# VectorE's share of the adaLN modulation as product-and-sum with a row of silu(c), and VectorE work per slot charged by durations

## The chip, the core and the metric

The kernel runs on one core of one Trainium2 chip. The metric is the device time of one execution in microseconds (us), lower is better. TensorE multiplies, VectorE and ScalarE work on tiles of 128 partitions, GpSimd is hardly used, and SyncE issues the weight loads from device memory.

## The reference, cut to what matters

Two layers; each has a token mixer (sparse attention, an S5 state-space branch, a pooling branch, merged by gates) and a convolutional FFN. Both sub-layers are modulated by shift, scale and gate vectors, which come from one vector c by a large matrix-vector product: per layer 6 parts of 2048 numbers.

```python
mod = silu(c) @ w_ada[l] + b_ada[l]        # (2048) x (2048, 12288), f32
sh1, sc1, g1, sh2, sc2, g2 = split(mod, 6)
h = rms_norm(x, g_norm1) * (1 + sc1) + sh1
x = x + g1 * hybrid_mixer(h, ...)          # attention, s5_mixer, pool_mixer, gates, w_out
h = rms_norm(x, g_norm2) * (1 + sc2) + sh2
x = x + g2 * conv_ffn(h, ...)
# in s5_mixer: y = gelu(scan(...)); y = y * sigmoid(y @ w_glu)
```

## The kernel before, in words

The large weights come as a stream of 936 slots, tiles of 128 x 1024 f32, in one order written out ahead. For each slot ScalarE makes a rounded copy (`whi`, `make_hi`), VectorE the remainder (`wlo`, `make_lo`), and TensorE multiplies: in the usual full slot eight 512-column matmuls with `whi` (line 326), then eight 256-column ones with `wlo` (line 331). There are three `wlo` buffers, so the `wlo` of slot s+2, which is made at the start of slot s, waits until TensorE is done with slot s-1. A slot is counted here by its `wlo` instruction.

All else is issued between slots by `step()`. Evacuations of finished outputs always run. Tasks are generators, stepped in a fixed order: first the low list (the modulation), then pooling, indexing, attention, and last S5 (`s5_task`). A task goes on only while `credit` > 0 (`step_task`, line 197). `credit` gains a fixed amount per slot (in proportion to its width) and is held between -2 and 2; every VectorE instruction, `wlo` and evacuations too, is charged by a formula in its helper (`tt`, `stt`, `ts`, `vcopy`). A piece that yields None ends the task's turn for that slot. If the stream comes to a block whose input isn't ready, `require()` steps the task that provides it at once and without regard to credit; everything it issues then stands ahead of that block on the engines' queues.

S5 has per layer 16 state groups in eight pairs: tables (`tb`, built by doubling on ScalarE and VectorE), two products of 512 columns, two of 256, two scans, three last products for each group, then matmuls (`prod,cc`). Every two pairs end in a tail (gelu, `yt`). The result y feeds the GLU (`w_glu`), at slot 160 in layer 0 and at slot 629 in layer 1. S5's tables of constants (`s5_prepare`, many short instructions) must be complete when the mixer opens (`open_mixer`, slot 37 in layer 0).

The modulation has 384 tiles of 128 x 1024 (`adaw`), loaded on SyncE's queue like the stream's weights; the list `ADA` sets their order and `ADA_PLAN` how many may be used by which slot (`ada_early`). 192 of them go through TensorE (`ada_group` with `on_pe`): four chunks side by side in one matmul step, not charged to credit, then a ScalarE copy `acc`, column transposes (line 569), small adds. The other 192 go through VectorE: per tile two passes `acc = w * c + acc` of 512 columns, and per eight tiles four transposes on TensorE and a reduction of their columns (line 545). The first 64 tiles use a ring of eight buffers, the later ones four.

Of the kernel before, what the change touches and what calls it, by code (L numbers as in the profile page):

```python
# [37 lines left out]
SLOT = 1024  # L38
NRAW, NHI, NLO, NADA, APRE = 4, 4, 3, 4, 4

# [39 lines left out]

ADA_PLAN = ((0, 18), (8, 34), (18, 50), (30, 66), (48, 66), (140, 128), (204, 160), (296, 192), (460, 296), (580, 320), (670, 356), (770, 384))


ADA = [(0, [(1, t), (0, t)], 2 if t < 4 else 4, True) for t in (0, 2, 4, 8, 12)]
for _l in range(DEPTH):
    if _l:
        ADA += [(_l, [(p, t + j) for j in (0, 4) for p in (1, 0)], 4, False) for t in (0, 8)]
    ADA += [(_l, [(2, t) for t in range(0, 16, 4)], 4, not _l)]
    ADA += [(_l, [(p, t + j) for j in (0, 4) for p in (4, 3)], 4, not _l or t == 0) for t in (0, 8)]
    ADA += [(_l, [(5, t) for t in range(0, 16, 4)], 4, False)]  # L90

# [29 lines left out]
class Kernel:  # L121
    def __init__(self, ctx, tc, a):
        self.tc, self.nc, self.a = tc, tc.nc, a
        nc = self.nc
        self.cpool = ctx.enter_context(tc.tile_pool(name="cpool", bufs=1))
        self.spool = ctx.enter_context(tc.tile_pool(name="spool", bufs=1))
        self.hpool = ctx.enter_context(tc.tile_pool(name="hpool", bufs=1))
        self.epool = ctx.enter_context(tc.tile_pool(name="epool", bufs=1))
        self.psum = ctx.enter_context(tc.tile_pool(name="psum", bufs=1, space=PSUM))
        self.slots = []  # L130
        self.tasks, self.low, self.evacs, self.fresh = [], [], [], []
        self.done = set()
        self.credit = 0.0
        self.acredit = 0.0
        self.banks = list(range(8))
        self.left = 0
        self.raw, self.hi, self.lo = {}, {}, {}
        self.slot_no = 0
        self.ada_tiles, self.ada_next, self.ada_on_pe = {}, 0, True
        dpool = ctx.enter_context(tc.tile_pool(name="dpool", bufs=1, space=bass.MemoryType.DRAM))  # L140
        self.x_save = dpool.tile([128, KT, T], F32, name="x_save")
        ctx.enter_context(tc.manual_schedule())

# [8 lines left out]
    def tt(self, out, a, b, op):  # L152
        self.credit -= 0.069 + 1.04e-3 * self.size(out)
        self.nc.vector.tensor_tensor(out, a, b, op=op)  # L154

    def stt(self, out, a, s, b, op0, op1):
        self.credit -= (0.069 if isinstance(s, float) else 0.13) + 1.04e-3 * self.size(out)
        self.nc.vector.scalar_tensor_tensor(out, a, s, b, op0=op0, op1=op1)  # L158

    def ts(self, out, a, s1, s2, op0, op1=None):  # L160
        self.credit -= 0.069 + 0.7e-3 * self.size(out)
        if op1 is None:
            self.nc.vector.tensor_scalar(out, a, s1, None, op0=op0)
        else:
            self.nc.vector.tensor_scalar(out, a, s1, s2, op0=op0, op1=op1)

    def vcopy(self, out, a):
        self.credit -= 0.069 + 0.7e-3 * self.size(out)
        self.nc.vector.tensor_copy(out, a)
# [209 lines left out]
    def run_stream(self):  # L379
        n = len(self.slots)  # L380
        for s in range(n):
# [6 lines left out]
            o.emit(self.hi.pop(s), self.lo.pop(s))  # L388
            self.credit = max(min(self.credit + 2.6 * o.w / SLOT, 2.0), -2.0)
            self.acredit = max(min(self.acredit + 2.6 * o.w / SLOT, 2.0), -2.0)  # L390
            self.step()
# [99 lines left out]
    def ada_fetch(self, upto):  # L491
        while self.ada_next < upto:
            i = self.ada_next
            pool, bufs = self.ada_ring if i < 64 and i % (NADA + APRE) < APRE else (self.cpool, NADA)
            t = pool.tile([128, 1024], F32, name="adaw", tag="adaw", bufs=bufs)
# [4 lines left out]
    def ada_group(self, i0, l, chunks, wt, on_pe, ahead, last):  # L500

        def mine(i, n):
            self.ada_fetch(min(i + n, last))
            return [self.ada_tiles.pop(i + j) for j in range(n)]
        m = len(chunks)
        self.ada_on_pe = on_pe
        if on_pe:
            b, ps = yield from self.take_bank()

            i, n, width = i0, wt // 2, 128 * wt  # L510
            for q in range(0, KT, 4 // m):
                ws = mine(i, n)
                for g in range(4):
                    k = q + g // m
                    cs = self.cact[:, k:k + 1].to_broadcast([128, 32])
                    w = ws[g * n // 4][:, g * width % 1024:][:, :width]
                    self.mm(ps[32 * g:32 * g + 32, :width], cs, w, start=q == 0, stop=q + 4 // m == KT)
                i += n
                self.ada_fetch(min(i + ahead, last))
                while self.ada_early(i):  # L520
                    yield None
                yield 1
        else:
            for g in range(m):
                acc = self.cpool.tile([128, 512], F32, name="acc", tag="acc", bufs=1)
                for q in range(8):
                    i = i0 + 8 * g + q
                    self.ada_fetch(min(i + ahead, last))
                    w, = mine(i, 1)
                    for k in range(2):  # L530
                        wk = w[:, k * 512:(k + 1) * 512]
                        cs = self.cact[:, 2 * q + k:2 * q + k + 1]
                        if q == 0 and k == 0:
                            self.ts(acc, wk, cs, None, OP.mult)
                        else:
                            self.stt(acc, wk, cs, acc, OP.mult, OP.add)
                        yield 1
                    while self.ada_early(i + 1):
                        yield None
                yield None  # L540
                b, cols = yield from self.ada_columns(acc, 4)
                part, t = chunks[g]
                mod = self.mod[l][:, 16 * part + t:16 * part + t + 4]
                self.credit -= 0.6
                self.nc.vector.reduce_sum(mod, cols, axis=AX.X)
                self.free_bank(b)
                self.ada_done(l, part, t, mod)
            return
        yield None
# [14 lines left out]
        yield None  # L564

    def ada_columns(self, acc, wt):
        b, ps = yield from self.take_bank()
# [11 lines left out]
    def ada_task(self, lo, hi, ahead, last):  # L579
        i = sum(2 * wt * len(chunks) for _, chunks, wt, _ in ADA[:lo])  # L580
        for l, chunks, wt, on_pe in ADA[lo:hi]:
            yield from self.ada_group(i, l, chunks, wt, on_pe, ahead, last)
            i += 2 * wt * len(chunks)
# [241 lines left out]
    def index_task(self, t):  # L825
# [34 lines left out]
        for r in range(TOPK // 8):  # L860
            self.nc.vector.max(m8, src)
            self.nc.vector.match_replace(wk[r % 2], m8, src, MARK)
            self.credit -= 2 * (0.069 + 1.04e-3 * nk)
            src = wk[r % 2]
# [7 lines left out]
    def attention_task(self, part):  # L872
# [7 lines left out]
        for t in range(2):  # L880
# [3 lines left out]
            for g in range(part, H // per, 2):  # L884
# [11 lines left out]
                self.free_bank(b)  # L896
                self.credit -= 0.6
                self.nc.vector.reduce_max(mxv[:, 0], lg, axis=AX.X)
# [154 lines left out]
    def s5_task(self):  # L1053
# [3 lines left out]
        for j in range(4):  # L1057
# [3 lines left out]
            for i0 in (0, 2):  # L1061
# [11 lines left out]
                for i, tb, (b, bu) in zip((i0, i0 + 1), tbs, bus):  # L1073
# [9 lines left out]
                    rb = p5.r[:, 4 * j + i:4 * j + i + 1].to_broadcast([128, T])  # L1083
                    self.credit -= 0.68
                    for c in range(2):
# [418 lines left out]
    def run(self):  # L1504
# [30 lines left out]
        self.ada_ring = pre, APRE  # L1535
        self.ada_fetch(APRE + NADA)
# [4 lines left out]
        self.norm(0, 1, self.x)  # L1541
        self.rope_tables(pre, posi)
        for s in range(3):
# [13 lines left out]
    def first_ada(self):  # L1557
        yield from self.ada_task(0, 2, APRE + NADA, 16)
        yield from self.ada_task(2, 5, APRE + NADA, 64)
        while ("open", 0) not in self.done:  # L1560
            yield None
        self.ada_fetch(64 + NADA)
        for _ in range(6):
# [49 lines left out]

def _ada(w, chunks, wt, by_k):

    w = w.reshape(KT, 128, 6, 2048)
    x = np.stack([w[:, :, part, 128 * t:128 * (t + wt)] for part, t in chunks])
    x = x.transpose(1, 0, 2, 3) if by_k else x
    return x.reshape(-1, 8 // wt, 128, 128 * wt).transpose(0, 2, 1, 3).reshape(-1, 128, 1024)
# [7 lines left out]
def _arrays(i):  # L1627
# [5 lines left out]
    o["pos"] = i["positions"][0].reshape(2, 128).T  # L1633
    o["w_ada"] = np.concatenate([_ada(i["w_ada"][l], chunks, wt, on_pe) for l, chunks, wt, on_pe in ADA])
    vecs, lvecs = [], []
# [75 lines left out]
```

## Time and profile before

| what | value |
|---|---|
| median of 3 runs | 2960.53 us (2960.5 to 2961.41) |
| profiled execution | 2961.13 us, span of its profile 2959.3 us |
| TensorE matmul busy | 2871.8 us, 97% |
| VectorE busy | 2316.7 us, 78% |
| ScalarE busy | 1385.9 us, 47% |
| mean granted clock of TensorE | 0.988 |

The span runs from the first to the last instruction of the profiled execution. Busy time is the time in which an engine works on at least one instruction; instructions of one engine overlap a little. PE is TensorE, DVE is VectorE, ACT is ScalarE; L154 is line 154 of the kernel printed above.

### The profile page before, as it was taken

The page shows a single profiled execution, that of the slowest core. Times are in us where ns is not written, and L with a number is a line of the kernel's source. Part 1 is how long each engine was busy: PE and PEld are TensorE (multiplying, and loading weights), DVE is VectorE, ACT ScalarE, POOL GpSimd, SP SyncE. Part 2 cuts the span into 40 slices and gives each one's busy share as a digit, 9 for nine tenths or more (in the row PEclk, how much of TensorE's full clock was granted, in tenths as well). Part 3 has the DMA queues.
Part 4 walks back from the last instruction along what each step waited for, and adds up shares of the span by engine and source line. Part 5 has one row for each costly group of instructions (what it writes and reads, how often), then busy time and mean ns, then how long its engine had stood idle before and what let it go on. Part 6 is the DMA issues. An engine that isn't in the chain of part 4 may idle for free.

```text
span 2959.3 us, 45094 instructions
## 1 busy us (share of the span) xinstructions
PE 2871.8 (97%) x16880; PEld 2431.4 (82%) x16880; DVE 2316.7 (78%) x4222; ACT 1385.9 (47%) x2209; POOL 43.6 (1%) x74
## 2 busy tenths in 40 slices
PE   6999999979999999999989999999999999999998
PEld 3787787758788888888868788888888888888887
DVE  5888677766698899999966887899888887556664
ACT  3355544434455543455434455555445554345542
POOL 0000000000000000000000000000000000000000
PEclk9999999989999999999999999999999999999999
DMA  9967767747677778888885555576676776555554
GB/s 368 351 221 254 239 235 259 247 144 277 207 257 252 254 274 295 294 283 302 299 300 198 197 180 181 192 244 239 246 267 207 241 236 204 187 191 187 189 193 151
DMA packets 195387, 705.97 MB, mean 239 GB/s; under 512 B 22496, under 2 KB 23008, under 8 KB 195168
## 3 DMA queue, kind: packets, MB, share of 16 engines
q1 hardware_dynamic: 190656, 691.23, 68.1%
q0 software_dynamic: 3648, 11.01, 1.0%
q8 instruction: 132, 2.16, 0.3%
q10 hardware_dynamic: 864, 0.86, 0.1%
q14 instruction: 87, 0.71, 0.1%
HBM read 698.82 MB, written 4.19 MB: 238 GB/s over the span
## 4 chain that ended last, share of the span: by engine, by line
PE 86%; issue 7%; DVE 5%; DMA 1%; ACT 0%; POOL 0%; POOLq 0%; SPq 0%; DVEq 0%; ACTq 0%
PE b L326 45%; PE b L331 23%; PE b L179 11%; PE b L355 6%; DVE wlo L154 2%; DMA adaw<-in_w_ada 1%; DVE acc L158 1%; PE b L569 0%; DVE prod L154 0%; DVE x L158 0%; POOL out L1497 0%; PE b L913 0%; DVE th L158 0%; DVE ftmp L154 0%; DVE m L154 0%
## 5 line engine op out<-in xcount | busy, mean ns | idle before, releaser
L154 DVE TENSOR_TENSOR wlo<-raw,whi 128x1024 fp32r<-128x1024 f32 x936 | 1136.9, 1215 | 509.9 <-PE b L331 252.8
L174 ACT ACTIVATE whi<-raw 128x1024 fp32r<-128x1024 f32 x936 | 980.8, 1052 | 914.3 <-PE b L326 443.7
L326 PE MATMUL b<-h,whi 128*128 128x512 f32 x4352 | 1104.5, 396 | 4.3 <-DVE h L158 4.3
L326 PEld LDWEIGHTS b<-h,whi 128*128 128x128 f32 x4352 | 784.6, 189 | 178.0 <-issue 18.7
L331 PEld LDWEIGHTS b<-h,wlo 128*128 128x128 f32 x4352 | 594.8, 191 | 43.7 <-DVE wlo L154 0.7
L331 PE MATMUL b<-h,wlo 128*128 128x256 f32 x4352 | 607.6, 282 | 0.3 <-DVE wlo L154 0.3
L326 PE MATMUL b<-hid,whi 128*128 128x512 f32 x1376 | 345.8, 393 | 3.2 <-DVE hid L158 3.2
L326 PEld LDWEIGHTS b<-hid,whi 128*128 128x128 f32 x1376 | 247.4, 189 | 49.1 <-DVE hid L158 4.1
L158 DVE SCALAR_TENSOR_TENSOR acc<-adaw,cact,acc 128x512 f32<-128x512 f32 x360 | 269.3, 748 | 5.2
L331 PEld LDWEIGHTS b<-hid,wlo 128*128 128x128 f32 x1376 | 187.6, 190 | 14.0 <-DVE wlo L154 0.7
L331 PE MATMUL b<-hid,wlo 128*128 128x256 f32 x1376 | 192.0, 282 | 0.3 <-DVE wlo L154 0.3
L179 PE MATMUL b<-whi,h 128*128 128x512 f32 (+1 forms) x512 | 155.2, 376 | 0.0
L326 PE MATMUL b<-mh,whi 128*128 128x512 f32 x512 | 130.7, 397 | 4.1 <-DVE mh L154 4.1
L174 ACT ACTIVATE fth<-ft 128x256 f32<-128x256 f32 x86 | 36.0, 418 | 199.1 <-DVE ft L158 199.1
L179 PE MATMUL b<-adaw,cact 128*32 128x512 f32 (+1 forms) x832 | 111.1, 582 | 9.0 <-DMA adaw<-in_w_ada 9.0
L179 PEld LDWEIGHTS b<-whi,h 128*128 128x128 f32 x512 | 94.1, 188 | 27.9 <-issue 9.5
L326 PEld LDWEIGHTS b<-mh,whi 128*128 128x128 f32 x512 | 92.6, 190 | 26.9 <-ACT whi L174 3.4
L179 PE MATMUL b<-wlo,h 128*128 128x512 f32 (+1 forms) x256 | 95.0, 371 | 0.0
L355 PE MATMUL b<-h,whi 128*128 128x256 f32 x384 | 78.1, 299 | 10.5 <-ACT whi L174 5.5
L174 ACT ACTIVATE hid<-ft 128x256 fp32r<-128x256 f32 x86 | 35.9, 418 | 108.9 <-DVE ft L154 108.9
L158 DVE SCALAR_TENSOR_TENSOR ft<-fa,lvecs,ft 128x255 f32<-128x255 f32 (+1 forms) x172 | 82.5, 481 | 3.0
L355 PEld LDWEIGHTS b<-h,whi 128*128 128x128 f32 x384 | 65.4, 205 | 15.7 <-ACT whi L174 6.6
(262 smaller groups left out, 2548.8 us busy)
## 6 DMA issues: line engine op xcount, KB each, us to landing
adaw<-in_w_ada SPq DMA_DIRECT2D x384, 512.0 KB, 5.5
raw<-in_w_up SPq DMA_DIRECT2D x344, 512.0 KB, 3.7
raw<-in_w_gate SPq DMA_DIRECT2D x192, 512.0 KB, 3.9
raw<-in_w_down_a SPq DMA_DIRECT2D x88, 512.0 KB, 3.5
raw<-in_w_down_b SPq DMA_DIRECT2D x84, 512.0 KB, 3.7
raw<-in_w_out SPq DMA_DIRECT2D x64, 512.0 KB, 4.4
raw<-in_w_q SPq DMA_DIRECT2D x32, 512.0 KB, 3.8
raw<-in_p_a SPq DMA_DIRECT2D x32, 512.0 KB, 4.4
```

What stands on the lines that cost most here:

```text
L154: self.nc.vector.tensor_tensor(out, a, b, op=op)
L158: self.nc.vector.scalar_tensor_tensor(out, a, s, b, op0=op0, op1=op1)
L174: self.nc.scalar.activation(out, a, func, bias=bias, scale=scale)
L179: self.nc.tensor.matmul(out, lhsT, rhs, start=start, stop=stop)
L326: self.nc.tensor.matmul(u.ps, hi[:, j * 128:(j + 1) * 128], x, start=u.cnt == 0, stop=False, skip_group_check=True)
L331: self.nc.tensor.matmul(u.ps[:, T:], lo[:, j * 128:(j + 1) * 128], x[:, :T], start=False, stop=last, skip_group_check=True)
L355: self.nc.tensor.matmul(ps, w, r, start=first and i == 0 and not u.after, stop=last and i == 2 and not u.before, skip_group_check=shared)
```

## The change

For VectorE's 192 tiles the weights are laid out transposed: output columns in partitions, 1024 of the 2048 inputs along the row. silu(c) is spread over all partitions as a row of 2048 by 16 small matmuls at the start, copied by ScalarE and stored in device memory (1 MB); half of it (512 KB) is loaded into one buffer whenever the half changes, seven times in all. One product-and-sum instruction per tile (`ada_sums`) gives 128 outputs' sums over 1024 inputs and adds them to the bias or to the first half's result; transposes, reduction and adds go. TensorE's groups with four chunks take half the width (`wt` 2), so a step uses one tile where it used two. After the first 64 tiles there are three tile buffers where there were four; the eighth of the first ring is the row's. The charges of VectorE instructions are raised, the slot's gain goes from 2.6 to 2.75, and the plan is adapted.

```diff
-NRAW, NHI, NLO, NADA, APRE = 4, 4, 3, 4, 4
+NRAW, NHI, NLO, NADA, APRE = 4, 4, 3, 3, 4
-ADA_PLAN = (..., (140, 128), (204, 160), (296, 192), (460, 296), (580, 320), (670, 356), (770, 384))
+ADA_PLAN = (..., (140, 128), (204, 160), (300, 192), (460, 288), (560, 310),
+            (660, 352), (765, 384))
...
+ADA = [(0, [(1, t), (0, t)], 2 if t < 4 else 4, None) for t in (0, 2, 4, 8, 12)]
+ADA += [(0, [(2, t + j) for j in (0, 2, 4, 6)], 2, None) for t in (0, 8)]
+ADA += [(0, [(p, t + j) for j in (0, 2) for p in (4, 3)], 2, None) for t in (0, 4, 8, 12)]
+ADA += [(0, [(5, t) for t in range(16)], 1, 0)]
+ADA += [(1, [(p, 8 * h + j) for j in range(8) for p in (1, 0)], 1, 1 - h) for h in range(2)]
+ADA += [(1, [(2, t) for t in range(16)], 1, 1)]
+ADA += [(1, [(p, t + j) for j in (0, 2) for p in (4, 3)], 2, None) for t in (0, 4)]
+ADA += [(1, [(p, 8 + j) for j in range(8) for p in (4, 3)], 1, 0)]
+ADA += [(1, [(5, t) for t in range(16)], 1, 1)]
...
     def tt(self, out, a, b, op):
-        self.credit -= 0.069 + 1.04e-3 * self.size(out)
+        self.credit -= 0.155 + 1.04e-3 * self.size(out)
     def stt(self, out, a, s, b, op0, op1):
-        self.credit -= (0.069 if isinstance(s, float) else 0.13) + 1.04e-3 * self.size(out)
+        self.credit -= (0.155 if isinstance(s, float) else 0.215) + 1.04e-3 * self.size(out)
     def ts(self, out, a, s1, s2, op0, op1=None):
-        self.credit -= 0.069 + 0.7e-3 * self.size(out)
+        self.credit -= (0.16 if isinstance(s1, float) else 0.215) + 0.55e-3 * self.size(out)
     def vcopy(self, out, a):
-        self.credit -= 0.069 + 0.7e-3 * self.size(out)
+        self.credit -= 0.15 + 0.6e-3 * self.size(out)
...
-            self.credit = max(min(self.credit + 2.6 * o.w / SLOT, 2.0), -2.0)
-            self.acredit = max(min(self.acredit + 2.6 * o.w / SLOT, 2.0), -2.0)
+            self.credit = max(min(self.credit + 2.75 * o.w / SLOT, 2.0), -2.0)
+            self.acredit = max(min(self.acredit + 2.75 * o.w / SLOT, 2.0), -2.0)
...
+    def ada_sums(self, i0, l, tiles, first, ahead, last):
+        i = i0
+        for h in (first, 1 - first):
+            self.ada_on_pe = False
+            if self.crow_half != h:
+                self.crow = self.cpool.tile([128, 1024], F32, name="crow", tag="crow", bufs=1)
+                self.nc.gpsimd.dma_start(self.crow, self.c_rows[:, h * 1024:(h + 1) * 1024])
+                self.crow_half = h
+                for _ in range(4):
+                    yield None
+            for part, t in tiles:
+                self.ada_fetch(min(i + ahead, last))
+                w = self.ada_tiles.pop(i)
+                n = 16 * part + t
+                col = self.mod[l][:, n:n + 1]
+                seed = self.vec(l, "b_ada")[:, n:n + 1] if h == first else col
+                self.credit -= 0.16 + 1.04e-3 * 1024
+                self.nc.vector.tensor_tensor_reduce(w, w, self.crow, 1.0, seed, OP.mult, OP.add, col)
+                if h != first:
+                    self.done.add(("mod", l, part, t))
+                i += 1
+                yield 1
+                while self.ada_early(i):
+                    yield None
...
+    def start_rows(self):
+        self.rows = []
+        for k in range(KT):
+            if k % 4 == 0:
+                self.rows.append(self.mm_bank())
+            self.mm(self.rows[-1][1][:, k % 4 * 128:k % 4 * 128 + 128], self.cact[:, k:k + 1].to_broadcast([128, 128]),
+                    self.ident)
+    def save_rows(self):
+        t = self.mx.tile([128, 2048], F32, name="rows", tag="oa")
+        for j, (b, ps) in enumerate(self.rows):
+            self.act(t[:, 512 * j:512 * j + 512], ps, AF.Copy)
+            self.free_bank(b)
+        self.nc.gpsimd.dma_start(self.c_rows, t)
+        self.crow_half = None
...
-            self.credit -= 2 * (0.069 + 1.04e-3 * nk)
+            self.credit -= 2 * (0.16 + 1.04e-3 * nk)
...
-                    self.credit -= 0.68
+                    self.credit -= 1.35
```

## Rows read from the trace of the kernel before

**Rows 1.** The page, part 1 (busy, share) and part 6 (KB, us to landing).

```profile
PE 2871.8 (97%) x16880; PEld 2431.4 (82%) x16880; DVE 2316.7 (78%) x4222; ACT 1385.9 (47%) x2209; POOL 43.6 (1%) x74
...
adaw<-in_w_ada SPq DMA_DIRECT2D x384, 512.0 KB, 5.5
```

**Rows 2.** Windows: length, PE, PEld, DVE, ACT, POOL busy (count), PEclk, DMA share, GB/s.

```profile
1100.00:1200.00 100.00, 99.68 (x575) 87.55 (x574) 96.88 (x187) 36.13 (x35) 0.00 (x0) 1.00 0.82 303
2500.00:2600.00 100.00, 100.00 (x573) 87.94 (x573) 56.33 (x64) 37.60 (x37) 0.00 (x0) 1.00 0.59 190
...
0.00:100.00 100.00, 71.77 (x472) 46.57 (x473) 61.57 (x229) 34.70 (x63) 2.14 (x7) 0.95 0.91 355
```

**Rows 3.** Waits of PE: us in total, times, longest.

```profile
PE b L179 <- DVE prod L154: 15.7, 4, 7.4
```

**Rows 4.** Timeline of PE from 1324 us: start, length, instructions merged [idle before].

```profile
1327.68 1.11 PE L331 MATMUL b<-h,wlo 128*128 128x256 f32 x8
1328.64 0.60 PE L569 MATMUL b<-const,acc 128*128 128x128 f32 x4
...
1330.92 1.12 PE L331 MATMUL b<-h,wlo 128*128 128x256 f32 x8
...
1333.71 1.12 PE L331 MATMUL b<-h,wlo 128*128 128x256 f32 x8
```

**Rows 5.** Timeline of PE from 447.6 us, a modulation step between two slots.

```profile
450.50 1.11 PE L331 MATMUL b<-h,wlo 128*128 128x256 f32 x8
451.55 1.06 PE L179 MATMUL b<-adaw,cact 128*32 128x512 f32 x8
...
454.49 1.11 PE L331 MATMUL b<-h,wlo 128*128 128x256 f32 x8
```

**Rows 6.** Timeline of PE from 34.5 us, a modulation group of half width.

```profile
35.75 3.66 PE L179 MATMUL b<-adaw,cact 128*32 128x256 f32 x64
39.34 0.50 PE L179 MATMUL b<-whi,h 128*128 128x512 f32 x1
```

**Rows 7.** Timeline of PE from 1517 us, the first steps of layer 1's group.

```profile
1519.52 1.11 PE L331 MATMUL b<-hid,wlo 128*128 128x256 f32 x8
...
1525.38 1.05 PE L179 MATMUL b<-adaw,cact 128*32 128x512 f32 x4 [2.90 <-DMA adaw<-in_w_ada]
...
1538.54 1.11 PE L331 MATMUL b<-hid,wlo 128*128 128x256 f32 x8
```

**Rows 8.** DVE's groups by form over the span: count, busy us, mean ns.

```profile
L154 DVE TENSOR_TENSOR wlo<-raw,whi 128x1024 fp32r<-128x1024 f32 x920 | 1123.8, 1222 | 498.9 <-PE b L331 252.8 <-issue 139.9 <-ACT fa L174 30.4
L158 DVE SCALAR_TENSOR_TENSOR acc<-adaw,cact,acc 128x512 f32<-128x512 f32 x360 | 269.3, 748 | 5.2
...
L1086 DVE TENSOR_TENSOR_SCAN prod<-r,prod 128x256 f32<-128x256 f32 x64 | 40.5, 675 | 0.0
```

**Rows 9.** Windows of the `wlo` instructions alone: length, DVE busy (count), PEclk, DMA.

```profile
175.33:606.76 431.43, 149.69 (x123) 1.00 0.72 247
1613.60:2067.80 454.20, 171.01 (x141) 1.00 0.62 206
```

**Rows 10.** Timeline of PE from 2060 us, S5's last matmuls in layer 1.

```profile
2065.81 1.91 PE L179 MATMUL b<-prod,cc 128*32 128x256 f32 x14 [0.60 <-DVE prod L154]
```

**Rows 11.** Timeline of DVE from 600 us, S5's rest in layer 0.

```profile
607.91 0.75 DVE L154 TENSOR_TENSOR prod<-prod 128x256 f32<-128x256 f32 x2
...
614.46 0.24 DVE L158 SCALAR_TENSOR_TENSOR tb<-tb,nsn,pr 128x16 f32<-128x16 f32 x1 [3.08 <-ACT pr L174]
...
626.84 1.14 DVE L154 TENSOR_TENSOR prod<-prod,tb 128x256 f32<-128x256 f32 x2
631.70 0.48 DVE L158 SCALAR_TENSOR_TENSOR yt<-u,lvecs,b 128x256 f32<-128x256 f32 x1 [3.71 <-PE b L179]
```

**Rows 12.** PE's groups by form over the span, S5's matmuls of both layers (16 pairs).

```profile
L179 PE MATMUL b<-prod,cc 128*32 128x256 f32 x256 | 36.2, 410 | 15.7 <-DVE prod L154 15.7
...
L179 PE MATMUL b<-u,bp 32*128 32x256 f32 x128 | 18.9, 403 | 0.1
```

More of the change, by code (lines that the diff above doesn't have):

```diff
@@ L79 @@
 FIRST = 48
[L81 to L90, printed above, removed]
+ADA_PLAN = ((0, 18), (8, 34), (18, 50), (30, 66), (48, 66), (140, 128), (204, 160), (300, 192), (460, 288), (560, 310),
+            (660, 352), (765, 384))
[8 more added lines that the diff above has]
+ADA += [(1, [(5, t) for t in range(16)], 1, 1)]
+ADA_FIRST = 64
 EARLY = ("oa", "big8", "qiT", "u", "m2k0", "m2k1", "pt0", "pt1")
@@ L141, in __init__ @@
         self.x_save = dpool.tile([128, KT, T], F32, name="x_save")
+        self.c_rows = dpool.tile([128, 2048], F32, name="c_rows")
         ctx.enter_context(tc.manual_schedule())
@@ L493, in ada_fetch @@
             i = self.ada_next
-            pool, bufs = self.ada_ring if i < 64 and i % (NADA + APRE) < APRE else (self.cpool, NADA)
-            t = pool.tile([128, 1024], F32, name="adaw", tag="adaw", bufs=bufs)
+            r = i % (APRE + NADA + 1) if i < ADA_FIRST else APRE
+            if r == APRE + NADA:
+                t = self.cpool.tile([128, 1024], F32, name="adaw", tag="crow", bufs=1)
+            else:
+                pool, bufs = self.ada_ring if r < APRE else (self.cpool, NADA)
+                t = pool.tile([128, 1024], F32, name="adaw", tag="adaw", bufs=bufs)
             self.nc.sync.dma_start(t, self.a["w_ada"][i])
@@ L498, in ada_fetch @@
             self.ada_next += 1
-    def ada_group(self, i0, l, chunks, wt, on_pe, ahead, last):
-        def mine(i, n):
-            self.ada_fetch(min(i + n, last))
[L504 to L539, printed above, removed]
-                yield None
[L541 to L548, printed above, removed]
@@ new lines, in ada_group @@
+    def ada_group(self, i0, l, chunks, wt, ahead, last):
+        m = len(chunks)
+        self.ada_on_pe = True
+        b, ps = yield from self.take_bank()
+        i, n, width = i0, wt // 2, 128 * wt
+        for q in range(0, KT, 4 // m):
+            self.ada_fetch(min(i + n, last))
+            ws = [self.ada_tiles.pop(i + j) for j in range(n)]
+            for g in range(4):
+                k = q + g // m
+                cs = self.cact[:, k:k + 1].to_broadcast([128, 32])
+                w = ws[g * n // 4][:, g * width % 1024:][:, :width]
+                self.mm(ps[32 * g:32 * g + 32, :width], cs, w, start=q == 0, stop=q + 4 // m == KT)
+            i += n
+            self.ada_fetch(min(i + ahead, last))
+            while self.ada_early(i):
+                yield None
+            yield 1
@@ L564, in ada_group @@
         yield None
+    def ada_sums(self, i0, l, tiles, first, ahead, last):
[9 more added lines that the diff above has]
+            for part, t in tiles:
+                self.ada_fetch(min(i + ahead, last))
+                w = self.ada_tiles.pop(i)
[7 more added lines that the diff above has]
+                i += 1
+                yield 1
+                while self.ada_early(i):
+                    yield None
[13 more added lines that the diff above has]
+        self.crow_half = None
     def ada_columns(self, acc, wt):
@@ L580, in ada_task @@
         i = sum(2 * wt * len(chunks) for _, chunks, wt, _ in ADA[:lo])
-        for l, chunks, wt, on_pe in ADA[lo:hi]:
-            yield from self.ada_group(i, l, chunks, wt, on_pe, ahead, last)
+        for l, chunks, wt, first in ADA[lo:hi]:
+            if first is None:
+                yield from self.ada_group(i, l, chunks, wt, ahead, last)
+            else:
+                yield from self.ada_sums(i, l, chunks, first, ahead, last)
             i += 2 * wt * len(chunks)
@@ L896, in attention_task @@
                 self.free_bank(b)
-                self.credit -= 0.6
+                self.credit -= 0.69
                 self.nc.vector.reduce_max(mxv[:, 0], lg, axis=AX.X)
@@ L1535, in run @@
         self.ada_ring = pre, APRE
-        self.ada_fetch(APRE + NADA)
+        self.ada_fetch(APRE + NADA + 1)
+        self.start_rows()
         for k in range(KT):
@@ L1541, in run @@
         self.norm(0, 1, self.x)
+        self.save_rows()
         self.rope_tables(pre, posi)
@@ L1557, in first_ada @@
     def first_ada(self):
-        yield from self.ada_task(0, 2, APRE + NADA, 16)
-        yield from self.ada_task(2, 5, APRE + NADA, 64)
+        yield from self.ada_task(0, 2, APRE + NADA + 1, 16)
+        yield from self.ada_task(2, 5, APRE + NADA + 1, ADA_FIRST)
         while ("open", 0) not in self.done:
             yield None
-        self.ada_fetch(64 + NADA)
+        self.ada_fetch(ADA_FIRST + NADA)
         for _ in range(6):
@@ L1611, in _wide, with _ada @@
     return np.ascontiguousarray(x.reshape(npc, per, 128, n).transpose(0, 2, 1, 3))
-def _ada(w, chunks, wt, by_k):
+def _ada(w, chunks, wt, first):
+    if first is not None:
+        w = w.reshape(2, 1024, 6, 16, 128)
+        return np.stack([w[h, :, part, t].T for h in (first, 1 - first) for part, t in chunks])
     w = w.reshape(KT, 128, 6, 2048)
-    x = np.stack([w[:, :, part, 128 * t:128 * (t + wt)] for part, t in chunks])
-    x = x.transpose(1, 0, 2, 3) if by_k else x
+    x = np.stack([w[:, :, part, 128 * t:128 * (t + wt)] for part, t in chunks]).transpose(1, 0, 2, 3)
     return x.reshape(-1, 8 // wt, 128, 128 * wt).transpose(0, 2, 1, 3).reshape(-1, 128, 1024)
@@ L1633, in _arrays @@
     o["pos"] = i["positions"][0].reshape(2, 128).T
-    o["w_ada"] = np.concatenate([_ada(i["w_ada"][l], chunks, wt, on_pe) for l, chunks, wt, on_pe in ADA])
+    o["w_ada"] = np.concatenate([_ada(i["w_ada"][l], chunks, wt, first) for l, chunks, wt, first in ADA])
     vecs, lvecs = [], []
```

## The prediction

> **What bounds the kernel now.** I read the page first: TensorE is busy for 97% of the span and VectorE for 78% [rows 1]. Then the windows: in a stretch where VectorE is 97% busy TensorE gets through 575 matmuls in 100 us, in one where VectorE is 56% busy through 573 [rows 2]. So in the FFN a busy VectorE costs nothing: TensorE sets the pace, and what VectorE saves there is not time. Next the waits of TensorE: the largest is 15.7 us on `prod`, the state-space task (S5) of layer 0 [rows 3]. So the question for each edit is: does it change TensorE's instructions, or what TensorE waits for where the stream meets a task that isn't done?
>
> **TensorE's instructions.** *Transposes.* 24 groups of four column transposes (one per VectorE chunk of eight tiles) go. A slot with such a group runs from lo to lo in 3.24 us, the next, plain one in 2.79 [rows 4]: 0.44 us each, -10.6 us. The eight short TensorE groups that stay have two transposes where four had four: +0.9 by the same price.
>
> *Steps of one tile.* The four TensorE groups with four chunks (128 tiles) worked in 64 steps of two tiles; now eight groups work in 128 steps of one. A slot with a two-tile step takes 454.49 - 450.50 = 3.99, so 1.20 more than a plain one [rows 5]. Sixteen tiles at half width in one run take 39.34 - 35.75 = 3.59 for eight steps of two chunks, 0.43 to 0.45 per tile [rows 6], so of the 1.20 about 0.34 is the price of coming and going. If each of the 64 extra steps stood alone: +22. Some fall together (after a group's evacuation the plan has moved two or three tiles on) or beside other small matmuls; half of that rebate leaves +16.5 (8 to 22).
>
> *The late group.* At 1520 us the layer-1 group starts eight tiles behind its plan, so five steps are issued in one slot, each waiting for its tiles: lo to lo 19.02 us against 2.79 + 5 x 1.20 [rows 7], so 10.3 lost. The new plan has 288 tiles at slot 460, where this group begins, and by the charges below VectorE can about keep it (0.6 tiles x 1.28 in 2.75 - 1.22 - 0.77 of a slot of the up-projection): -10.3 (0 if it falls behind in the pauses for the row).
>
> *Start.* 16 small matmuls and four ScalarE copies lie under the wait for x and the first tiles. The row's store adds 1 MB where DMA is 91% busy at 355 GB/s [rows 2]: 0 to 3, taken +2. The seven later row loads stand on GpSimd's queue, each behind the last sum that reads the old half; behind them stand only the small S5 and pool loads, x, x_save and the rsqrt, and none of these is due then. The first sum after a load comes four slots (11 us) on; such a 512 KB load lands in 5.5 [rows 1]. Three tile buffers for four: a load is asked two sums ahead, over three slots (9 us) at 0.6 tiles per slot, also above 5.5; SyncE's wait for that buffer stands before weight loads that wait for a later `wlo` anyway. Nothing for either, unless sums bunch: then `wlo` queues behind a late sum and TensorE behind that.
>
> **The new VectorE sum.** No row shows it. At least it costs what a 1024-wide two-input pass does, 1.22 (`wlo`), at most two of these, 2.44 [rows 8]. It has two fp32 inputs, as the 512-wide `acc` pass has (748 ns, 1.04 ns an element beyond 0.215), so I take 1.28; two such passes and a share of the reduction are replaced, some 0.25 us a tile. That is 47 us of VectorE work, and by rows 2 worth nothing by itself. [...]
>
> **The charges.** This is the largest part. A task's next piece is issued only while `credit` > 0. Until now a slot brought 2.6 and an instruction was charged less than it takes; now a slot brings 2.75 and the charges equal the durations (scan pair 0.68 before, 1.35 now, measured 2 x 675 ns; `wlo` 1.134 before, 1.220 now, measured 1222) [rows 8]. S5 gains least: a pair of state groups has 16 `tb` passes of 16 to 128 columns, and for each of two groups two 512-wide and two 256-wide products, two scans, and three last products: 10.7 by the old charges, 14.6 by the new; a tail per four groups 1.3 and 1.6. Eight pairs and four tails per layer: 91 before, 123.5 now.
>
> *Layer 1, slots 488 to 628* (141 `wlo` [rows 9]). Old supply 141 x 2.6 = 367, spent whole; less `wlo` 160 and S5 91, other work was 116. That is mostly 256-wide passes, 0.335 before and 0.421 now: 145; 35 `acc` passes and their ends in it (31) become some 19 sums (23): 138. New supply 388, less `wlo` 172, less 138: 78 for S5's 123.5. So 45 is left when the stream reaches the GLU, which needs y; before nothing was left, TensorE waited 0.60 us for the last `prod` [rows 10]. *Layer 0, slots 37 to 159* (123 [rows 9]): old supply 319, `wlo` 139; S5 had 76, since the trace shows 14.7 (20 by the new charges) drained at the GLU from 607.9 on [rows 11]; other work 103, now 130. New supply 337 - 150 - 130 = 58: 66 left against 20, +46; if some 12 of the old supply was lost at the cap of 2 (attention waits between 326 and 369 us), +31. I take +38 and, by the same doubt, 41 for layer 1 (35 to 45).
>
> What is left is issued at once when the GLU asks for it, behind a `wlo` that waits for the slot before, so TensorE stands. There a pair takes from 611.4, before the 3.08 wait of `tb`, to 628.0: 16.6 us [rows 11]. Its matmuls (2.26 + 1.18 per pair [rows 12]) then cost the stream nothing: 13.2 net. A tail takes from 628.0 to 634.2 with its 3.71 wait for TensorE, some 4.4 beyond its charge. Layer 0: 38/14.6 = 2.6 pairs, 34, and half a tail more: +36 (28 to 45). Layer 1: 41/14.6 = 2.8 pairs, 37, and a tail more: +42 (32 to 48). *S5's tables* of layer 0 are due when the mixer opens at slot 37, after 33 slots worth 31 full ones. They are short passes, by the two price lists 22 before and 36 now; old supply 81 less `wlo` 35 and 22 leaves 24 of other work, about 32 now; 86 - 38 - 32 = 16 for 36. 17 to 20 is left, in passes that overlap, with three slots of `wlo` already made as cover (10 us): +3 (0 to 11).
>
> What is late next: VectorE now idles some 0.3 us of each mixer slot while S5 waits for credit. Nothing later gives this back, since the output projection needs all of it.
>
> **Sum.** -10.6 + 0.9 + 16.5 - 10.3 + 2 + 36 + 42 + 3 = +79.5 on the profiled execution's 2961.1 (span 2959.3 and 1.8 around it): 3040.6; the median lies 0.6 below that execution: **3040**. All low ends give +48 (3009), all high ends +119 (3080).
>
> **Rivals.** *The charges don't hold S5* (the other side): if S5 is held by banks and its chain through TensorE and ScalarE, not by credit, then the GLU waits as long as before; -10.6 + 0.9 + 16.5 - 10.3 + 2 = -1.5, 2959, and with the extra steps at 8 us 2951. It decides once less than about 9 us of work is added at the two GLUs. Against it: the gaps in VectorE's work of the mixers are small while S5 has work, and S5 ends just in time in layer 1 as a supply that is spent whole would make it. *Half of it*: attention, which stands ahead of S5, leaves slack that S5 takes up, or one layer alone waits: +40 - 1.5, about 3000. [...]
>
> **How the numbers follow.** Forecast 0.72; half of it 0.10; slow sum 0.06; charges that hold nothing 0.12, of which 0.07 faster and 0.05 within 0.2% (6 us, about what a measurement of this kernel tells from no change). So slower 0.88. 2990 to 3085 holds the forecast's bounds and most of the half case, and leaves out the rest.
>
> **What would show it.** Right: TensorE's wait on `prod` grows from 15.7 to some 70 us, in stands of about 70 us before the GLU of layer 0 and 50 before that of layer 1, with several pairs of groups in each; VectorE less busy in the mixers before them; 32 column transposes for 128; a slot with a one-tile step at 3.56; no 19 us slot before layer 1; 192 sums of about 1.28. Wrong: the last scans of a layer close before its GLU as now; sums near 2.4 and `wlo` among TensorE's waits; the layer-1 group late again.

## The result, and the profile of the changed kernel

The changed kernel takes 3071.07 us (median of 4 runs, 3068.71 to 3072.53) against 2960.55 for the kernel before, measured beside it: ratio 1.0372 (95% interval 1.0354 to 1.039). The forecast was slower, 3040, in 2990 to 3085: the sign and the range held, the point was 31 us short.

The page, parts 1 and 5, of the changed kernel (count, busy us, mean ns, idle time before):

```profile
PE 2909.7 (95%) x17328; PEld 2454.6 (80%) x17328; DVE 2285.2 (74%) x4190; ACT 1393.1 (45%) x2217; POOL 48.0 (2%) x82
...
L567 DVE CUSTOM_DVE_ANT_0 adaw<-adaw,crow,mod 128x1024 f32<-128x1024 f32 x96 | 122.5, 1279 | 10.0 <-DMA adaw<-in_w_ada 9.7
...
L186 PE MATMUL b<-prod,cc 128*32 128x256 f32 x256 | 48.4, 481 | 71.7 <-DVE prod L161 71.7
```

VectorE is less busy than before, 74% for 78%, and so is TensorE, 95% for 97% [rows 1]. L567 is the new sum. Its groups by form say what VectorE's instructions cost:

```profile
L161 DVE TENSOR_TENSOR wlo<-raw,whi 128x1024 fp32r<-128x1024 f32 x920 | 1124.5, 1223 | 606.4 <-PE b L338 271.6 <-issue 198.9 <-ACT whi L181 31.7
...
L1115 DVE TENSOR_TENSOR_SCAN prod<-r,prod 128x256 f32<-128x256 f32 x64 | 40.5, 674 | 0.0
...
L567 DVE DVE_READ_ACCUMULATOR2_ANT mod<- 128x1 f32 x192 | 15.8, 82 | 0.0
```

The durations of before stand unchanged (1222 and 675 ns [rows 8]): these VectorE instructions did not become slower. What changed is who waits. The waits of TensorE (us in total, times, longest), where before had 15.7 in 4 for `prod` [rows 3]:

```profile
PE b L186 <- DVE prod L161: 71.7, 13, 10.1
PE b L186 <- DVE wlo L161: 10.1, 1, 10.1
PE b L186 <- DMA adaw<-in_w_ada: 9.2, 13, 3.1
PE b L186 <- ACT pt L181: 7.6, 5, 3.1
...
PE b L942 <- DVE lg L170: 5.0, 3, 2.7
```

To find where, I cut the span at the same `wlo` passes in every kernel (the pass for slot s + 2 opens slot s). These are the windows of the `wlo` passes alone of the changed kernel from slot 0 on, cut at slots 36, 38, 96, 100, 160, 162, 208, 463, 466, 628 and 630: length, VectorE busy with `wlo` (count), granted clock, DMA share, GB/s.

```profile
31.07:172.24 141.17, 41.58 (x38) 0.97 0.85 329
172.24:191.00 18.76, 2.06 (x4) 0.90 0.49 171
191.00:392.36 201.36, 70.25 (x58) 0.98 0.70 236
392.36:432.58 40.22, 4.91 (x4) 0.75 0.33 108
432.58:645.94 213.36, 73.33 (x61) 0.98 0.72 242
645.94:717.44 71.50, 2.45 (x2) 0.62 0.06 23
717.44:865.41 147.97, 56.35 (x46) 1.00 0.76 257
865.41:1590.38 724.97, 311.33 (x255) 0.99 0.82 280
1590.38:1600.04 9.66, 3.67 (x3) 1.00 0.93 342
1600.04:2127.61 527.57, 194.74 (x162) 0.99 0.65 211
2127.61:2190.09 62.48, 2.44 (x3) 0.62 0.07 23
2190.09:3070.19 880.10, 372.11 (x304) 0.99 0.66 213
```

The table gives the length of each stretch before and, for the changed kernel and six of the experiments, how much longer it is.

| slots | before, us | changed | charges only | early rate | old charges | mixer rate | old modulation | rate steps |
|---|---|---|---|---|---|---|---|---|
| start to 36 | 172.7 | -0.4 | -0.7 | +1.5 | +0.3 | +0.9 | +1.3 | +3.0 |
| 36 to 38 (tables) | 6.5 | +12.2 | +12.2 | -0.3 | 0.0 | -0.3 | -0.3 | -0.3 |
| 38 to 96 | 204.7 | -3.4 | -8.5 | +5.9 | +5.1 | +6.4 | +3.3 | +11.4 |
| 96 to 100 (oc) | 15.7 | +24.5 | +17.5 | +8.6 | +2.0 | +9.9 | -0.9 | +4.1 |
| 100 to 160 | 207.1 | +6.2 | -4.4 | +7.0 | +11.5 | +12.0 | +1.1 | +13.1 |
| 160 to 162 (GLU) | 36.6 | +34.9 | +33.4 | +8.0 | -3.5 | -23.3 | -18.8 | -30.2 |
| 162 to 208 | 143.5 | +4.4 | +2.3 | +5.7 | +3.8 | +3.4 | +0.2 | +3.4 |
| 208 to 463 (FFN) | 733.8 | -8.9 | -3.9 | -8.8 | -1.0 | -8.1 | -3.1 | -9.1 |
| 463 to 466 | 24.6 | -14.9 | -16.2 | -15.7 | -16.2 | -15.4 | -16.2 | -14.3 |
| 466 to 628 | 520.3 | +7.2 | +20.6 | +8.6 | +8.9 | +19.2 | +30.3 | +19.3 |
| 628 to 630 (GLU) | 11.1 | +51.4 | +68.2 | +50.8 | +0.7 | -7.5 | +0.3 | -7.7 |
| 630 to end | 882.6 | -2.5 | -2.3 | -2.8 | -1.4 | +0.1 | +0.8 | -0.3 |
| span | 2959.3 | +110.9 | +118.1 | +68.2 | +10.3 | -2.5 | -1.9 | -7.7 |

Four places make +123 in the changed kernel: slot 37, where S5's tables are due, slots 96 to 100, where the stream needs the pools' `oc`, and the two GLUs, which need S5's y. A fifth stand hides in the stretch from 466 to 628, slot 548, where the stream needs layer 1's `oc`. Windows of the `wlo` pass that opens it, first in the kernel before, then in the changed one:

```profile
1819.47:1823.99 4.52, 1.23 (x1) 1.00 0.63 221
...
1867.16:1884.99 17.83, 1.22 (x1) 0.90 0.24 86
```

It is 13.3 us longer. The whole stretch grew by 7.2 alone; what S5 has not issued by slot 628 does not take TensorE's time there. TensorE at the first GLU:

```profile
645.77 0.62 PE L186 MATMUL b<-prod,cc 128*32 128x256 f32 x2
650.60 2.83 PE L186 MATMUL b<-prod,cc 128*32 128x256 f32 x14 [4.20 <-DVE prod L161]
...
662.05 1.06 PE L186 MATMUL b<-prod,cc 128*32 128x256 f32 x2 [6.62 <-DVE prod L161]
666.63 3.62 PE L186 MATMUL b<-prod,cc 128*32 128x256 f32 x14 [3.51 <-DVE prod L161]
...
681.64 1.06 PE L186 MATMUL b<-prod,cc 128*32 128x256 f32 x2 [9.38 <-DVE prod L161]
686.21 3.27 PE L186 MATMUL b<-prod,cc 128*32 128x256 f32 x14 [3.51 <-DVE prod L161]
...
698.12 1.06 PE L186 MATMUL b<-prod,cc 128*32 128x256 f32 x2 [7.58 <-DVE prod L161]
702.69 3.56 PE L186 MATMUL b<-prod,cc 128*32 128x256 f32 x14 [3.51 <-DVE prod L161]
708.82 0.39 PE L362 MATMUL b<-yh,whi 128*128 128x256 f32 x1 [2.56 <-ACT yh L181]
```

Each pair of state groups ends with one `x14`; four fall into the stand, the first partly made before it. A pair takes 16.0 us (650.60 to 666.63) to 16.5 (686.21 to 702.69), as [rows 11] priced it (16.6). How much of S5 is left at a GLU can be counted by its scans, four per pair and 32 per layer. Windows of the scans alone (VectorE busy, count) at the two GLUs, first in the kernel before, then in the changed one:

```profile
606.77:643.35 36.58, 3.80 (x6) 0.72 0.13 44
2065.67:2076.75 11.08, 0.00 (x0) 1.00 0.32 96
...
645.94:717.44 71.50, 8.86 (x14) 0.62 0.06 23
2127.61:2190.09 62.48, 7.60 (x12) 0.62 0.07 23
```

So 3.5 pairs are left at layer 0's GLU where 1.5 were, and 3 at layer 1's where none was.

### The profile page after: what moved, and what is told of

It reads as the page before. It is cut to its first block, busy times and chain, and to the rows that moved or that the text cites. A ratio compares the mean times of both kernels' runs of the same rounds, so it can differ in the third digit from the quotient of the medians.

```text
span 3070.2 us, 45972 instructions
## 1 busy us (share of the span) xinstructions
PE 2909.7 (95%) x17328; PEld 2454.6 (80%) x17328; DVE 2285.2 (74%) x4190; ACT 1393.1 (45%) x2217; POOL 48.0 (2%) x82
## 4 chain that ended last, share of the span: by engine, by line
PE 88%; DVE 5%; issue 3%; ACT 1%; DMA 1%; POOL 0%; POOLq 0%; ACTq 0%; SPq 0%; DVEq 0%
PE b L333 47%; PE b L338 24%; PE b L186 11%; PE b L362 5%; DVE prod L161 1%; DVE wlo L161 1%; DMA adaw<-in_w_ada 1%; DVE prod L1115 1%; DVE tb L165 0%; DMA raw<-in_w_qi 0%; ACT pr L181 0%; POOL out L1526 0%; DVE m L161 0%; PE b L942 0%; DVE prod L165 0%
## 5 line engine op out<-in xcount | busy, mean ns | idle before, releaser
L333 PEld LDWEIGHTS b<-h,whi 128*128 128x128 f32 x4352 | 783.8, 189 | 177.6 <-ACT whi L181 17.3
L567 DVE CUSTOM_DVE_ANT_0 adaw<-adaw,crow,mod 128x1024 f32<-128x1024 f32 x96 | 122.5, 1279 | 10.0 <-DMA adaw<-in_w_ada 9.7
L186 PE MATMUL b<-adaw,cact 128*32 128x256 f32 (+1 forms) x1344 | 118.3, 428 | 9.3 <-DMA adaw<-in_w_ada 9.2
L567 DVE CUSTOM_DVE_ANT_0 adaw<-adaw,crow,vecs 128x1024 f32<-128x1024 f32 x96 | 122.4, 1278 | 2.7 <-DMA adaw<-in_w_ada 2.7
L186 PE MATMUL b<-prod,cc 128*32 128x256 f32 x256 | 48.4, 481 | 71.7 <-DVE prod L161 71.7
L186 PE MATMUL b<-wlo,h 128*128 128x512 f32 (+1 forms) x256 | 96.1, 376 | 10.1 <-DVE wlo L161 10.1
L186 PEld LDWEIGHTS b<-prod,cc 128*32 128x32 f32 x256 | 17.7, 131 | 97.7 <-DVE prod L161 80.6
L362 PE MATMUL b<-h,whi 128*128 128x256 f32 x384 | 79.2, 302 | 11.1 <-ACT whi L181 6.1
```

The costliest lines, as they stand in the source:

```text
L186: self.nc.tensor.matmul(out, lhsT, rhs, start=start, stop=stop)
L333: self.nc.tensor.matmul(u.ps, hi[:, j * 128:(j + 1) * 128], x, start=u.cnt == 0, stop=False, skip_group_check=True)
L362: self.nc.tensor.matmul(ps, w, r, start=first and i == 0 and not u.after, stop=last and i == 2 and not u.before, skip_group_check=shared)
L567: self.nc.vector.tensor_tensor_reduce(w, w, self.crow, 1.0, seed, OP.mult, OP.add, col)
```

## The experiments

The theory (T1): the new charges against 2.75 starve the tasks, which then drain by force where the stream needs them. Its rival (R1): the new modulation itself costs the time.

**Charges only.** The kernel before with the seven changed charges (six are in the diff above; the seventh, attention's 0.6, becomes 0.69) and 2.75, nothing else.

> The kernel before with the new charges and 2.75 credit per slot alone; the modulation stays as it was. If the charges make the time (T1): S5, the tables and attention fall behind, drains as in the changed kernel (some 12 us at slot 37, 24 at slots 96 to 100, 35 and 51 at the two GLUs), TensorE's wait on prod some 70 us, time about 3075 (3050 to 3095). If the new modulation itself costs the time (R1: the sums, the row's loads, three buffers, the one-tile steps): within 10 us of the kernel before, 2960.

3080.9 us, ratio 1.04 (1.0384 to 1.0415). The loss is there without the new modulation, in the same four stretches (column "charges only"). R1 falls as the cause.

**Old charges.** The changed kernel with these seven charges and 2.6 as before.

> The changed kernel with the old charges and 2.6 credit per slot (the sum keeps its own charge of 1.22). T1: the drains go, the rest of the change stays (transposes about -10, late group -15 to 0, one-tile steps +8, start +2): about 2950 (2935 to 2965), wait on prod back to some 16 us. R1: about 3070, as the changed kernel.

2971.42, ratio 1.0035 (1.0021 to 1.0049). The drains are gone; 10 us stay, not the -10 expected. The column shows why: +5, +11 and +4 in layer 0's mixer, where the one-tile steps are. TensorE also waits 7.9 us there for `adaw` tiles, which the kernel before does not.

**Rates of 3.05 and 3.4**, in the changed kernel:

```diff
-            self.credit = max(min(self.credit + 2.75 * o.w / SLOT, 2.0), -2.0)
-            self.acredit = max(min(self.acredit + 2.75 * o.w / SLOT, 2.0), -2.0)
+            self.credit = max(min(self.credit + 3.05 * o.w / SLOT, 2.0), -2.0)
+            self.acredit = max(min(self.acredit + 3.05 * o.w / SLOT, 2.0), -2.0)
```

> The changed kernel with its new charges, but 3.05 credit per slot in place of 2.75 (about what VectorE's durations add up to in a mixer slot of the kernel before, 3.04 us). T1: some 28 us of S5 left at the first GLU and 10 at the second instead of 59 and 43, so drains shrink to about a third: about 2985 (2960 to 3010). R1: 3070, the rate does nothing.

> The changed kernel with its new charges and 3.4 credit per slot (about the real length of a slot of the mixers, 3.3 to 3.5 us). T1: S5 and attention are done when asked for; what stays is the change of the modulation: about 2945 (2930 to 2965), unless tasks that run too early make wlo late: then TensorE waits on wlo and the time lies between 2960 and 3000. R1: 3070.

3007.14 (1.0154; 1.0139 to 1.0169) and 2966.17 (1.0016; 1.0006 to 1.0025). With 3.05, slots 628 to 630 are 13.8 us longer than before in place of 51.4: 0.3 x 141 slots = 42.3 of supply bought 37.6 us, 0.89 each, where the prediction's 13.2 of 14.6 is 0.90. That they meet is in part luck: 37.6 is the whole stand, 13.2 is net of S5's matmuls. At 3.4 everywhere slots 208 to 463 lose 4.2 in place of gaining 8.9: VectorE is overfilled there, TensorE waits for `wlo` 8.8 us in 11 places between 1040 and 1210 us.

**Mixer rate.** 3.4 in the mixers alone:

```diff
+            rate = 3.4 if s < 210 or 466 <= s < 678 else 2.75
-            self.credit = max(min(self.credit + 2.75 * o.w / SLOT, 2.0), -2.0)
+            self.credit = max(min(self.credit + rate * o.w / SLOT, 2.0), -2.0)
```

> The changed kernel with 3.4 credit per slot in the mixers (slots 0 to 209 and 466 to 677) and 2.75 elsewhere. With 3.4 everywhere TensorE lost 12 us between slots 300 and 380, in layer 0's FFN, some of it waiting for wlo. If that is VectorE overfilled with sums by the rate (T1): it goes, and the time is about 2956 (2948 to 2962). If it has another cause (the two-sum distance of the tiles, the DMA): 2966, as with 3.4 everywhere.

2958.52, ratio 0.9985 (0.9976 to 0.9995). The FFN is back at -8.1: it was the rate there.

**Pairs.** The same, with two one-tile steps in one visit:

```diff
             self.ada_fetch(min(i + ahead, last))
+            if m == 4 and wt == 2 and q % 2 == 0:
+                continue
             while self.ada_early(i):
```

> The kernel of the mixer rate (3.4 in the mixers, 2.75 elsewhere), in which the four-chunk TensorE groups of two-tile chunks issue two one-tile steps together, 64 visits in place of 128, as the kernel before did. If the 64 extra visits cost what the prediction took for them (16.5, 8 to 22): 8 to 22 us under the mixer-rate kernel, about 2940. If the visits' price is made good elsewhere (TensorE would have stood in those slots anyway): within 4 us of it, about 2956.

2964.4, ratio 1.0005 (0.9996 to 1.0015): neither. TensorE's timeline shows both halves:

```profile
499.74 0.61 PE L186 MATMUL b<-adaw,cact 128*32 128x256 f32 x8
504.31 0.64 PE L186 MATMUL b<-adaw,cact 128*32 128x256 f32 x8 [3.95 <-DMA adaw<-in_w_ada]
504.88 3.39 PE L333 MATMUL b<-oa,whi 128*128 128x512 f32 x8
...
519.97 2.00 PE L333 MATMUL b<-h,whi 128*128 128x512 f32 x8
521.81 1.11 PE L338 MATMUL b<-h,wlo 128*128 128x256 f32 x8
522.86 1.07 PE L186 MATMUL b<-adaw,cact 128*32 128x256 f32 x16
523.86 2.11 PE L333 MATMUL b<-h,whi 128*128 128x512 f32 x8
525.80 1.12 PE L338 MATMUL b<-h,wlo 128*128 128x256 f32 x8
```

A pair that has its tiles makes a slot of 525.80 - 521.81 = 3.99, 1.20 more than a plain one [rows 4]. But the second tile is often not there: waits for `adaw` are 26.5 us in all, 12.9 in the mixer-rate kernel. These and the slower matmuls behind them (the row of 3.39 above) outweigh the saving. There are three buffers, where the kernel before, with the same steps, has four; their number was not varied alone.

**Plan only.** The kernel before with the new `ADA_PLAN`.

> The kernel before with the new points of the plan alone (300, 192; 460, 288; 560, 310; 660, 352; 765, 384). If the points make the late group of layer 1 start in time (the old ones ask for 296 tiles at slot 460, where the group that begins at tile 288 can't have begun): the 19 us slot goes, -10 to -16, about 2946. If it is the cheaper sum that brings VectorE to its tiles in time: the group stays late, 2955 to 2961.

2965.7, ratio 1.001 (1.0001 to 1.0019). The late group's 14.6 us do go with the plan, but slots 208 to 463 grow by 13.6, and nearly all of that is one slot, 302. VectorE and TensorE there:

```profile
1065.00 0.68 DVE L546 TENSOR_REDUCE mod<-b 128x4 f32<-128x512 f32 x1
1066.31 10.22 DVE L159 SCALAR_TENSOR_TENSOR acc<-adaw,cact,acc 128x512 f32<-128x512 f32 x13
...
1080.56 2.07 PE L332 MATMUL b<-hid,wlo 128*128 128x256 f32 x8 [6.93 <-DVE wlo L155]
```

The down-projection asks here for the whole gate of layer 0's FFN (`need_mod`). With the later plan point (300 for 296) the gate's last chunk lacks only its reduction. By the code a forced turn ends only where the task yields None, and that comes at a chunk's end: after the reduction it runs on through 16 `acc` passes (11.8 us) of layer 1's first chunk, which nobody has asked for yet. The next `wlo` stands behind them. In the kernel before, the gate was complete in time, and that chunk's passes lie one or two to a slot. So the loss is a chunk that just misses its due, and the plan alone makes the late group go.

**Early rate.** The changed kernel with `rate = 3.4 if s < 105 else 2.75`.

> The changed kernel with 3.4 credit per slot up to slot 104 and 2.75 behind it. T1: the 12 us at slot 37 go and the 25 us at slots 96 to 100 shrink to some 12, so 33 us late at slot 104 becomes about 15; S5 stands behind attention and gets none of it, so 35 and 51 us at the two GLUs stay: about 3053 (3045 to 3060). Rival: what is not drained early is lacking later, since the same supply is only spent earlier: the first GLU takes it back, 3071.

3030.94, ratio 1.0234 (1.0218 to 1.0249). The drains at 37 and 96 shrank as expected, but so did the first GLU's, from 34.9 to 8.0, against the expectation that S5 gets nothing while attention stands ahead of it. In slots 37 to 104 the extra supply is 0.65 x 67 = 43.6; the two stretches together gave back 15.9 + 26.9 = 42.8, while slots 38 to 96 took 9.3 more. S5 did get credit: when slot 104 opens, 10 of its scans have been issued, 4 in the changed kernel. This fits the code, where a task that waits for its own bank or matmul ends its turn and lets the next one have the credit; no run isolates it.

**Split steps.** The kernel before, each two-tile step in two visits:

```diff
                 for g in range(4):
+                    if n == 2 and g == 2:
+                        yield 1
+                        while self.ada_early(i + 1):
+                            yield None
                     k = q + g // m
```

> The kernel before, with each two-tile step of its four TensorE groups issued as two visits of one tile (two 512-wide matmuls each), the second when the plan asks for its tile: 64 visits more, everything else as before. If a visit has a price of its own, as the prediction took it (0.34 each, less what falls together: +16.5, 8 to 22): 2968 to 2983, about 2977. If the prediction's price was a mistake of the view and TensorE only does the same matmuls at another time: within 4 us of 2961.

3025.94, ratio 1.0217 (1.0203 to 1.0231): 64 us, four times the expectation. TensorE's timeline:

```profile
508.54 1.11 PE L331 MATMUL b<-oa,wlo 128*128 128x256 f32 x8
...
512.59 1.11 PE L331 MATMUL b<-oa,wlo 128*128 128x256 f32 x8
513.63 1.05 PE L179 MATMUL b<-adaw,cact 128*32 128x512 f32 x4
...
516.56 1.11 PE L331 MATMUL b<-h,wlo 128*128 128x256 f32 x8
```

Half a step, four records of 512 columns in two blocks of 32 output rows, takes 1.05 us; the whole one, eight records in four blocks, took 1.06 [rows 5]. The slot is 516.56 - 512.59 = 3.97 against 3.99. So four blocks take 0.01 us more than two, and half the matmuls cost the whole time, 1.18 a slot. Counted in the traces, 108 visits stand for 53 in slots 38 to 96, 100 to 160, 162 to 208 and 466 to 628: 55 x 1.18 = 65, and these stretches grew by 63. The run does not price a visit alone, since it doubles TensorE's time for the columns as well.

**Rate of 4.2** in the mixers:

> The changed kernel with 4.2 credit per slot in the mixers (above the longest slots, so credit holds nothing there) and 2.75 elsewhere. If what is left of the forced drains at slots 96 to 104 (some 10 us with 3.4) still comes from credit (T1): they go, the time falls 5 to 10 us under the kernel with 3.4, about 2950. If pooling and attention are then held by their own chains through TensorE and ScalarE: no gain, 2956 to 2960; if the tasks then stand before wlo, TensorE's wait on wlo grows and it is over 2960.

2958.92, ratio 0.9986 (0.9977 to 0.9995): slots 96 to 100 fell to +3.9, and the start grew to +5.8, so nothing is gained over 3.4 (2958.52).

**Old modulation at the mixer rate.** The charges-only kernel with the rates 3.4 and 2.75 of the mixer-rate kernel.

> The kernel before (its modulation, its plan, four buffers) with the new charges and the rates of the mixer-rate kernel: 3.4 in the mixers, 2.75 elsewhere. It tells what the new modulation is worth once the charges hold nothing. If the charges were the whole loss and the new modulation gives what the prediction's other terms sum to (about nothing, -1.5): 2958 to 2964. If the new modulation earns something at a good rate (late group and transposes outweigh the one-tile steps): 2965 to 2972. If it costs (the one-tile steps outweigh): 2940 to 2955, and this is the best kernel.

2958.66, ratio 0.9989 (0.998 to 0.9998), the same as with the new modulation. Once no task starves, the new modulation is worth nothing in sum against the old one with its old plan: in layer 0's mixer (38 to 96, 100 to 160, 162 to 208) it costs 21.8 where the old one costs 4.6. In the FFN it saves 5.0 more (-8.1 for -3.1), and behind slot 466 another 11.1 (+19.2 for +30.3): there the old plan's group is late again, 16 tiles in a row from 1609.39 to 1632.06 us, 22.7 where eight two-tile steps at 1.20 take 9.6. The old modulation with the new plan at these rates was not run, so what the new one is worth against a plan that fits stays open.

**Rate steps.** 3.4 up to slot 36, 4.2 in the mixers behind it, 2.75 elsewhere, in the changed kernel.

> The changed kernel with 3.4 credit per slot up to slot 36, 4.2 in the mixers behind it and 2.75 elsewhere. With 4.2 from the start 5 us were lost before slot 36, and 2954 was still the span. If those 5 us come from the tables' passes standing before wlo (T1) they go: 2946 to 2954. If not: 2959, as with 4.2 from the start.

2953.7, ratio 0.997 (0.9959 to 0.9981): 8 us under the kernel before (2961.72 beside it), the best here. The windows of its `wlo` passes at the two GLUs:

```profile
638.00:644.40 6.40, 2.45 (x3) 1.00 0.61 210
...
2065.96:2069.31 3.35, 2.36 (x3) 1.00 0.88 304
```

No stand is left at either: 6.40 us where the changed kernel has 71.50.

## Why the prediction was right, and where its sum was off

The mechanism was the forecast's: supply per slot against charges, work left over, issued by force. Charges alone make the loss; the old charges, or a higher rate, take nearly all of it away. The signs it named are there: 71.7 us of wait on `prod` where it named some 70, several pairs of groups in both stands, no late slot before layer 1, and in the timeline of TensorE in the changed kernel a slot with a one-tile step of 477.14 - 473.58 = 3.56:

```profile
473.58 1.11 PE L338 MATMUL b<-oa,wlo 128*128 128x256 f32 x8
474.62 0.64 PE L186 MATMUL b<-adaw,cact 128*32 128x256 f32 x8
...
477.14 1.11 PE L338 MATMUL b<-h,wlo 128*128 128x256 f32 x8
```

In the table, the measured column is that of the stretches above. A stretch can hold more than its term, as the paragraphs below say.

| term | predicted | measured |
|---|---|---|
| transposes, net (208 to 463, 630 to end) | -9.7 | -11.4 |
| one-tile steps (38 to 96, 100 to 160, 162 to 208, 466 to 628) | +16.5 | +14.4 |
| late group (463 to 466) | -10.3 | -14.9 |
| start | +2 | -0.4 |
| tables at slot 37 | +3 | +12.2 |
| drain at slots 96 to 100 | none | +24.5 |
| layer-0 GLU | +36 | +34.9 |
| layer-1 GLU | +42 | +51.4 |

**The missing term** is the drain of attention at slots 96 to 100. The prediction let S5 carry the whole shortfall, since it stands last. But attention and pooling have dues of their own, half way through layer 0's mixer, and by then the supply was short for them too. (The code lists `oc` among what attention provides, so the demand for it forces attention as well as pooling.) In the changed kernel their softmax passes stand in a row from 390 us on, with TensorE waiting for `lg` and `pt` in the waits above. This is the largest part of the 31 us. Layer 1 has the same drain at slot 548, 13.3 us more; the table hides it in the row of the one-tile steps.

**The tables** were sized nearly right: 17 to 20 left by the prediction, and VectorE works on their passes from 175.67 to 191.00, 15.3 us, before the next `wlo`:

```profile
175.67 0.22 DVE L176 CAST ftmp<-ftmp 128x128 int32<-128x128 f32 x1
...
191.00 1.23 DVE L161 TENSOR_TENSOR wlo<-raw,whi 128x1024 fp32r<-128x1024 f32 x1
```

What failed is the cover. The prediction set three made slots, 10 us, against the passes. TensorE waited 10.1 us for that `wlo`, so it had work for some 6 us of them, and the stretch grew by 12.2.

**The GLU of layer 0** came out near its price, +34.9 for +36, by two errors that cancel. Two more pairs were left than before, not 2.6; the drain at slots 96 to 100 had taken part of the shortfall, as it seems. But the price took 3.4 us a pair off for S5's own matmuls, and these are missing from earlier stretches, not from the stand: two pairs at 16.0 to 16.5 are 32 to 33.

**The GLU of layer 1** was 9 low mainly for that second reason, not for more work. Three pairs were left, where the prediction took 2.8; priced whole, its own 2.8 x 16.6 + 4.4 is 50.9 against 51.4. What the matmuls save stands in the stretch from 466 to 628: +7.2 there, +19.2 in the mixer-rate kernel, where S5 is done in time. That the old modulation leaves still more (+68.2) fits the prediction's 138 against 145.

**The one-tile steps.** Their +14.4 in the changed kernel is not their price: the drain at slot 548 is in it, and the matmuls of tasks that starve are not. Visits counted in the traces are 110 for 53 in the same stretches, 57 more, where +16.5 stands for 48 at 0.34. At equal rates layer 0's three stretches give 21.8 - 4.6 = 17.2 for 36 more visits (79 for 43), with nearly the same other matmuls. Of that, 5.0 us are waits for `adaw`, which the old modulation does not have there; the other 12.2 are 0.34 a visit. So the price was right, the rebate for steps that fall together was too large, and 57 x 0.34 = 19 lies inside the range. The waits for tiles are a term that the prediction put at nothing; whether three buffers make them is not shown. The run in [rows 6] is eight tiles, not sixteen as the prediction says; its price per tile is right.

**The late group** was read rightly as a matter of the plan: the plan alone takes it away.

**The slow sum**, to which the forecast gave 0.06, falls: no run shows one near 2.4 us; the sum takes 1279 ns against 1.28 us predicted, and a read of 82 ns behind it. The two rivals fall as well: the charges held S5, and both layers waited.

## What to carry to other kernels

Charges and supply act by their ratio: whoever raises the charges to the true durations must raise the supply by what the tasks took before, stage by stage, and not to the length of a plain slot, since a slot with tasks in it is longer (here 3.56 us with a one-tile step and 3.99 with a two-tile one [rows 5], against 2.79 [rows 4]). To price such a change, list every place where the stream demands a task's result, not the last task only, and work out the shortfall at each. Look also at how far a forced turn runs: one that ends only at a chunk's end can issue much that nobody asked for. A step's small matmuls are to be priced as the trace shows them, before they are cut into smaller steps: here by the columns that go through (512 columns take 1.05 us in two blocks and 1.06 in four, 256 in four take 0.64) and by some 0.34 us per visit.

## What the runs showed of the hardware that was not expected

For matmuls with 32 weight columns the number of blocks of 32 output rows hardly counted: with 512 columns, two blocks (four records) take 1.05 us in the split-steps kernel, four (eight records) 1.06 [rows 5]. What the 0.34 us per visit consist of, no run here separates.

In the stands TensorE was slow. In the first GLU's stretch the mean granted clock is 0.62, where the rate-steps kernel, which has no stand there, has 1.00. The four `x14` were granted 0.65, 0.50, 0.57 and 0.53 and took 2.83 to 3.62 us, where [rows 10], at 1.00, has 1.91. Behind the 3.95 us wait in the pairs kernel the next eight matmuls take 3.39, where eight of the same shape from 519.97 us on take 2.00: with these 1.39 us, as it seems, the wait cost more than its length.

The sum with a written total is two records: 1279 ns and a read of the accumulator of 82 ns, 15.8 us in all. The prediction had only the first.
